# A two-layer streaming trunk: seven block products for eight in each projection group, and the plain eight

## The chip, the cores and the metric

The kernel runs on one core of one Trainium2 chip. The metric is the device time of one execution in microseconds (us); for a comparison, the median over several executions. Everything is computed in fp32. Where a product must be exact to nearly fp32, an operand is split into a high part in the fast fp32r format and a low part that holds the rest, and three matmuls (high x high, high x low, low x high) make one product.

## The reference

256 rows of 2048 numbers pass through two layers. Layer A is chunked attention with a relative-position bias; layer B is attention with a forget gate and a causal mask, against keys and values made from the stream once. Both gate the result with SiLU and project it back.

```python
D_MODEL, SEQ, D_INNER, N_HEADS, HEAD_DIM = 2048, 256, 4096, 32, 128
# layer A
h = rms_norm(x, a_norm[0])
q, k, v, g = jnp.split(h @ a_w_in[0], 4, axis=-1)        # 2048 -> 4 x 4096
o = chunked_relbias_attention(q, k, v, a_rel_bias[0])    # 64-row chunks, own and earlier ones
x = x + (o * jax.nn.silu(g)) @ a_w_out[0]                # 4096 -> 2048
# shared keys and values, forget gates
h_kv = rms_norm(x, kv_norm)
k_sh, v_sh = jnp.split(h_kv @ kv_w, 2, axis=-1)
cum_logf = jnp.cumsum(jax.nn.log_sigmoid(h_kv @ f_w + f_b), axis=1)
# layer B
q, g = jnp.split(rms_norm(x, b_norm[0]) @ b_w_in[0], 2, axis=-1)
o = forgetting_attention(q, k_sh, v_sh, cum_logf)        # causal
x = x + (o * jax.nn.silu(g)) @ b_w_out[0]
return rms_norm(x, final_norm)
```

## The kernel before

The weights are streamed once, in units of 512 output columns. A unit holds 16 slices of 128 rows of the inner dimension (32 in the output projections), taken two at a time: a sub-block is 256 x 512 numbers, 512 KB. `Feed` brings them: `load` starts the transfer on SP's queue into one of three raw buffers (`RAW`), `prepare` makes the high part on ScalarE (ACT) and the low part on VectorE (DVE) into one of four pairs of split buffers (`SPLIT`), and `get` hands a pair to TensorE (PE), with up to three pairs made ahead (`DEPTH`). `Unit.step` then multiplies: two slices, two halves of 128 rows of x, three matmuls each, so 12 matmuls of 128 x 512 for a sub-block, accumulated in two PSUM banks.

Both layers run over 16 groups of two heads (`NG`), two units for a group. In layer A these are aqk (queries and keys) and avg (values and gates); in layer B bqg (queries and gates, from `b_w_in`) and bkv (keys and values, from `kv_w`). The output projections ao and bo (`project`) stand behind the layers.

From the second group of each layer on, the units have only seven sub-blocks (`QUAD * KB` slices). The eighth sub-blocks of the two units of a group form a quad: two slices of two units against two halves of rows, which is a 2 x 2 block matrix times another, done in seven block products in place of eight. `Quads` holds what is needed. `load_quad` fetches both raw sub-blocks ahead of time, ordered by a dummy activation (`behind`); `differ` forms differences of weight blocks on DVE (in layer B it scales them by the gain on ACT first); `quad` splits four tiles of such combinations on ACT and DVE; `sums_of_x` forms the sums of x once per layer; `products` issues the seven products (21 matmuls) behind the third step of the group's first unit, four into banks of their own (p1, p5, p6, p7), and combines them on DVE and ACT into the tile `comb`. When a unit ends, `first_half` (L650) and `whole_sums` (L656) add `comb` to the accumulators on DVE. The first group of each layer has plain units of eight sub-blocks, whose evacuation is `evac_scaled` on ACT (L414).

Attention is a generator, cut by `yield` into segments that `drive` calls between the steps of the units, so that the work of one group lies beside the matmuls of the next. Its parts, in order:

- `turn(qk)`: a DVE transpose (L405) and 16 small transfers (L408) from POOL's queue, in layer A four of them from ACT's; target is `home`, a space inside the quad's tiles
- the split of keys and queries (wide, q1, q0) on ACT and DVE
- s1p and s0p: scores on PE, then the softmax on DVE and ACT, in two segments
- gates and `turn(sg)`: four activations, a transpose, 16 transfers on POOL's queue into sgZ
- the split of the probabilities (wideh on ACT L427, widel on DVE L428), ordered by a dummy activation behind the split of a coming sub-block (`line`)
- op: values times probabilities on PE (L435 to L437, L493)
- oT: gate and split of the result

Step tables say behind which sub-block a segment is called: in layer A `PV7_STEPS` and `QK7_STEPS`, in layer B `B1_STEPS` and `B2_STEPS`. `drive` also takes the generator of the group before that (`old`): one segment (the split of the probabilities) is called behind step 0, and everything left, op first, behind step 1. PE works in this written order: it cannot pass an op that waits. On the other engines the order is set when the program is laid out, near the order of the calls, and is fixed on the chip.

## Time and profile before

| | us |
|---|---|
| median of three runs | 1816.73 |
| lowest and highest run | 1811.34, 1823.83 |
| the profiled execution, whole | 1826.52 |
| its span, first to last instruction | 1824.8 |
| PE busy in it | 1771.9 |
| DVE busy | 1420.1 |
| ACT busy | 1184.8 |
| POOL busy | 522.0 |

The stages of the span: the first group of layer A to about 53.7 us, its 15 quad groups to 730.7, the first output projection to 899.1, the first group of layer B to 948.2, its 15 quad groups to 1640.3, and the second output projection with the final norm to 1824.8. The granted TensorE clock has a mean of 0.988 of full speed over the execution.

A row of a timeline gives start, length, engine, line, operation, output and inputs, shape and count; a bracket tells how long the engine stood idle before it and for whom. A row of the waits gives the waiting instruction, the one that released it, the sum in us, how often, and the longest. A line can be that of a helper: L184 is every unit's matmul, L435 to L437 every product of three.

### The profile page before, as it was taken

Reading aid. Unit: us, or ns where it says so; the run is one execution under the profiler, and the core shown is the slowest. Engines: PE = TensorE matmul, PEld = TensorE weight load, DVE = VectorE, ACT = ScalarE, POOL = GpSimd, SP = SyncE. Lnnn points to the kernel's source line nnn. Section 1 sums busy time; section 2 is a strip of 40 time slices with the busy share of each in tenths; the row PEclk is TensorE's granted clock in tenths of the full one; section 3 lists DMA queues with packets and bytes.
Section 4 is the critical chain, followed back from the end, with each engine's and each line's share of the span. In section 5 each row is a group of like instructions: output and inputs, shape, how many; then the busy total and the mean of one; then the engine's idle time right before and its main releaser. Section 6 shows DMA issues by size and latency. Waiting matters only on the chain.

```text
span 1824.8 us, 26015 instructions
## 1 busy us (share of the span) xinstructions
PE 1771.9 (97%) x8297; PEld 1534.1 (84%) x8297; DVE 1420.1 (78%) x2094; ACT 1184.8 (65%) x2245; POOL 522.0 (29%) x1071
## 2 busy tenths in 40 slices
PE   9999999999999999999999999999999999999997
PEld 7888888888888888888888888888888888888886
DVE  7888888888887787665668888888888889886554
ACT  6666666666566566554557877777777778765443
POOL 1333333333333333222014333333333333333000
PEclk9999999999999999999999999999999999999999
DMA  8776676666666666677756666666666666666664
GB/s 276 224 226 218 216 227 218 219 218 224 219 217 214 219 204 204 211 242 246 234 188 217 216 215 216 218 215 215 215 216 213 213 209 219 206 224 215 214 213 159
DMA packets 151337, 396.38 MB, mean 217 GB/s; under 512 B 31104, under 2 KB 38560, under 8 KB 151072
## 3 DMA queue, kind: packets, MB, share of 16 engines
q1 hardware_dynamic: 115152, 354.25, 59.4%
q0 software_dynamic: 32256, 37.29, 6.7%
q10 hardware_dynamic: 3792, 3.17, 0.6%
q8 instruction: 66, 1.08, 0.3%
q14 instruction: 71, 0.58, 0.1%
HBM read 351.05 MB, written 4.23 MB: 195 GB/s over the span
## 4 chain that ended last, share of the span: by engine, by line
PE 29%; DMA 13%; DVE 12%; ACT 7%; issue 4%; POOL 0%; ACTq 0%; SPq 0%; DVEq 0%
PE ao_acc L184 8%; PE bo_acc L184 7%; PE bqg_acc L184 6%; DMA bkv_raw<-in_kv_w 4%; DVE bqg_lo L241 3%; DMA bqg_raw<-in_b_w_in 3%; DVE bkv_lo L241 2%; PE bkv_acc L184 2%; ACT bkv_hi L240 2%; DMA cb<-cumd 2%; ACT bqg_hi L240 1%; DVE quad_lo L286 1%; DVE qk L650 1%; DMA bo_raw<-in_b_w_out 1%; PE op L493 1%
## 5 line engine op out<-in xcount | busy, mean ns | idle before, releaser
L408 POOL DMA_DIRECT2D sgZ<-sgY x512 | 251.4, 498 | 510.6 <-issue 245.9
L245 ACT ACTIVATE avg_hi<-avg_raw 128x1024 fp32r<-128x1024 f32 x112 | 118.3, 1056 | 137.9 <-DMA avg_raw<-in_a_w_in 88.7
L241 DVE SCALAR_TENSOR_TENSOR bkv_lo<-bkv_raw,gain,bkv_hi 128x512 fp32r<-128x512 f32 x226 | 159.2, 743 | 44.9 <-ACT bkv_hi L240 44.8
L246 DVE TENSOR_TENSOR avg_lo<-avg_raw,avg_hi 128x1024 fp32r<-128x1024 f32 x112 | 136.7, 1220 | 59.1 <-ACT avg_hi L245 59.0
L241 DVE SCALAR_TENSOR_TENSOR bqg_lo<-bqg_raw,gain,bqg_hi 128x512 fp32r<-128x512 f32 x226 | 163.5, 770 | 14.7 <-ACT bqg_hi L240 14.4
L240 ACT ACTIVATE bqg_hi<-bqg_raw,gain 128x512 fp32r<-128x512 f32 x226 | 148.4, 710 | 38.1 <-DMA bqg_raw<-in_b_w_in 27.7
L184 PE MATMUL bqg_acc<-bqg_hi,x1Th 128*128 128x512 f32 x452 | 173.0, 394 | 0.0
L184 PE MATMUL bqg_acc<-bqg_lo,x1Th 128*128 128x512 f32 x452 | 169.6, 387 | 0.0
L184 PE MATMUL bqg_acc<-bqg_hi,x1Tl 128*128 128x512 f32 x452 | 169.4, 386 | 0.0
L184 PE MATMUL aqk_acc<-aqk_hi,xTh 128*128 128x512 f32 x452 | 168.3, 384 | 1.0 <-ACT aqk_hi L245 1.0
L240 ACT ACTIVATE bkv_hi<-bkv_raw,gain 128x512 fp32r<-128x512 f32 x226 | 149.8, 711 | 29.4 <-DMA bkv_raw<-in_kv_w 26.0
L184 PE MATMUL avg_acc<-avg_hi,xTh 128*128 128x512 f32 x452 | 168.0, 383 | 0.0
L184 PE MATMUL aqk_acc<-aqk_lo,xTh 128*128 128x512 f32 x452 | 166.8, 381 | 1.2 <-DVE aqk_lo L246 1.2
L184 PE MATMUL aqk_acc<-aqk_hi,xTl 128*128 128x512 f32 x452 | 166.8, 381 | 0.0
L184 PE MATMUL avg_acc<-avg_lo,xTh 128*128 128x512 f32 x452 | 166.6, 380 | 0.0
L184 PE MATMUL avg_acc<-avg_hi,xTl 128*128 128x512 f32 x452 | 166.5, 380 | 0.0
L184 PE MATMUL bkv_acc<-bkv_hi,x1Th 128*128 128x512 f32 x452 | 166.3, 379 | 0.0
L184 PE MATMUL bkv_acc<-bkv_hi,x1Tl 128*128 128x512 f32 x452 | 166.1, 379 | 0.0
L184 PE MATMUL bkv_acc<-bkv_lo,x1Th 128*128 128x512 f32 x452 | 166.1, 379 | 0.0
L408 POOL DMA_DIRECT2D b_sums<-b_quad x256 | 125.7, 499 | 137.9 <-issue 62.6
L246 DVE TENSOR_TENSOR aqk_lo<-aqk_raw,aqk_hi 128x1024 fp32r<-128x1024 f32 x110 | 131.9, 1222 | 41.1 <-ACT aqk_hi L245 40.9
L408 POOL DMA_DIRECT2D sums<-quad x192 | 94.5, 499 | 195.1 <-PE op L493 173.3
(318 smaller groups left out, 4392.6 us busy)
## 6 DMA issues: line engine op xcount, KB each, us to landing
bqg_raw<-in_b_w_in SPq DMA_DIRECT2D x113, 512.0 KB, 4.2
bkv_raw<-in_kv_w SPq DMA_DIRECT2D x113, 512.0 KB, 4.7
avg_raw<-in_a_w_in SPq DMA_DIRECT2D x112, 512.0 KB, 5.6
aqk_raw<-in_a_w_in SPq DMA_DIRECT2D x110, 512.0 KB, 4.0
ao_raw<-in_a_w_out SPq DMA_DIRECT2D x64, 512.0 KB, 4.1
bo_raw<-in_b_w_out SPq DMA_DIRECT2D x64, 512.0 KB, 4.2
sgZ<-sgY POOLq DMA_DIRECT2D x512, 40.0 KB, 4.0
quad<-in_a_w_in SPq DMA_DIRECT2D x32, 512.0 KB, 6.2
```

The costliest lines, as they stand in the source:

```text
L184: pe.matmul(acc[t], x[:, t * P:(t + 1) * P], w, start=t not in begun, stop=k == nk - 1 and i == 2)
L240: act.activation(hi[:, :, j], raw[:, :, j], AF.Copy, scale=gk)
L241: dve.scalar_tensor_tensor(lo[:, :, j], raw[:, :, j], gk, r32(hi[:, :, j]), op0=OP.mult, op1=OP.subtract)
L245: act.activation(hi[:, :, j], raw[:, :, j], AF.Copy)
L246: dve.tensor_sub(lo[:, :, j], raw[:, :, j], r32(hi[:, :, j]))
L286: dve.tensor_sub(lo[:, :, :n], src, r32(hi[:, :, :n]))
L408: queues[j].dma_start(out=r32(z)[j * SQ:(j + 1) * SQ, i], in_=y[i * SQ:(i + 1) * SQ, j])
L493: pe.matmul(op[:, i, P:], v1[:, i * DH:(i + 1) * DH], pT[:, i, NT], start=False, stop=i == HG - 1)
L650: dve.scalar_tensor_tensor(dst[:, t], acc[t][:, :dst.shape[-1]], rs[:, t:t + 1], self.comb[:, i0 + t, :dst.shape[-1]], op0=OP.mult, op1=OP ...
```

## The change

The quads go in both layers. All units have eight sub-blocks, and `Feed` knows only these: `load_quad`, `differ`, `quad` and the class `Quads` are left out, with their big tiles. One tile, `turned`, takes over the space that `turn(qk)` used inside the quads' tiles, for both layers. All groups evacuate with `evac_scaled` on ACT, and the v and gate parts are read from PSUM directly. The step tables are written for eight steps, and `drive` takes a table for the older generator too: in layer A op is now called behind step 2, in layer B still behind step 1.

```diff
-PV_STEPS = {0: 1, 7: 1}
-QK7_STEPS = {0: 1, 5: 1, 6: 2}
-PV7_STEPS = {0: 1}
-B1_STEPS = {2: 1, 3: 1, 5: 2}
-B2_STEPS = {0: 1}
+PV_STEPS = {1: 1}
+OLD_A_STEPS = {0: 1, 2: 99}
+B1_STEPS = {3: 1, 5: 1, 6: 2}
+B2_STEPS = {1: 1}
+OLD_B_STEPS = {0: 1, 1: 99}
+FORGET_STEPS = {0: 1, 2: 1, 6: 1, 7: 1}
...
-        nk = KD if g == 0 else QUAD * KB
-        qkvg.append(spec(f"aqk{g}", a_w_in[2 * g], nk))
-        qkvg.append(spec(f"avg{g}", a_w_in[2 * g + 1], nk))
+        qkvg.append(spec(f"aqk{g}", a_w_in[2 * g], KD))
+        qkvg.append(spec(f"avg{g}", a_w_in[2 * g + 1], KD))
...
+    turned = big_tile([P, 2, NQ, 2 * HG * NT, SQ], F32, name="turned")
+    home = [turned[:, i] for i in range(2)]
...
         qk = rows(UN, "qk")
-        if g:
-            qa.first_half(qk, accs["qk"], 0, rsA)
-        else:
-            evac_scaled(accs["qk"], 0, UN, rsA, qk)
+        evac_scaled(accs["qk"], 0, UN, rsA, qk)
...
-    def drive(gen, side, steps, hooks={}, old=None, last=0):
+    def drive(gen, side, steps, hooks={}, old=None, old_steps={}):
         acc = None
         for i, acc in enumerate(gen):
-            finish(old) if i >= last else advance(old)
+            advance(old, old_steps.get(i, 0))
             advance(side, steps.get(i, 0))
...
-            first, second = (Unit(xT, next(order)) for _ in range(2))
-            accs["qk"] = drive(rest(first), prev, PV7_STEPS,
-                               {QUAD_STEP - 1: lambda: qa.products(first, second, (rsA, [(t, UN) for t in range(NT)])),
-                                LOAD_STEP: lambda: g + 1 < NG and feed.load_quad("a", g + 1)})
-            vg = rest(second)
+            accs["qk"] = drive(unit(xT), prev, PV_STEPS)
+            vg = unit(xT)
...
-        accs["vg"] = drive(vg, prev, QK7_STEPS, {0: lambda: g + 1 < NG and feed.differ("a")}, old, 1)
-        if not g:
-            qa.sums_of_x()
+        accs["vg"] = drive(vg, prev, QK_STEPS, {}, old, OLD_A_STEPS)
...
-    project(oA, ao_order, ao_begun, ao_closed, [(prev, [1, 7, 1, 1])])
+    project(oA, ao_order, ao_begun, ao_closed, [(prev, [2, 6, 2, 1])])
...
-        if g:
-            qb.first_half(qk[:, :, GC:], kv, NT, rsB)
-            kv = qb.whole_sums(kv, NT, GC)
-        else:
-            evac_scaled(kv, 0, GC, rsB, qk[:, :, GC:])
+        evac_scaled(kv, 0, GC, rsB, qk[:, :, GC:])
...
-        accs["qg"] = drive(rest(first), prev, B1_STEPS, hooks, old, 1)
-        hooks = {2: lambda: open_b(accs), 3: lambda: more and feed.differ("b")}
-        accs["kv"] = drive(rest(second), prev if g else fg, B2_STEPS if g else {1: 1, 3: 1, 6: 1, 7: 1}, hooks)
+        accs["qg"] = drive(unit(x1T), prev, B1_STEPS, {}, old, OLD_B_STEPS)
+        accs["kv"] = drive(unit(x1T), prev if g else fg, B2_STEPS if g else FORGET_STEPS, {2: lambda: open_b(accs)})
...
-    project(oB, bo_order, bo_begun, bo_closed, [(old, [1, 1, 0]), (prev, [3, 1, 1, 1, 1, 7, 1, 1])])
+    project(oB, bo_order, bo_begun, bo_closed, [(old, [1, 1, 0]), (prev, [4, 2, 1, 1, 1, 7, 2, 1])])
```

`QK_STEPS = {0: 1, 6: 1, 7: 2}` stands in both versions; only the new one uses it.

149 lines of the change are left out of this document (15 added, 134 removed).

## The prediction

> **What bounds the kernel.** I read the page's busy shares first, then the stages (windows), the waits of PE, and the timelines of PE, DVE and ACT around the longest wait.
>
> ```profile
> PE 1771.9 (97%) x8297; PEld 1534.1 (84%) x8297; DVE 1420.1 (78%) x2094; ACT 1184.8 (65%) x2245; POOL 522.0 (29%) x1071
> ```
> ```profile
> 53.70:730.70 677.00, 666.02 (x3139) 575.76 (x3137) 549.47 (x732) 420.14 (x763) 208.98 (x435) 0.99 0.68 217
> ```
> ```profile
> 948.20:1640.30 692.10, 668.46 (x3129) 581.37 (x3127) 595.35 (x991) 530.40 (x1117) 252.98 (x509) 0.98 0.65 214
> ```
>
> The two windows are the 15 quad groups of each layer (columns: length, then busy time of PE, PEld, DVE, ACT, POOL, granted clock, DMA share, GB/s). PE is called 97% busy, but the matmul rows overlap, so that share hides lost time. The price of a matmul is the distance between starts; in the kv unit below (first row to the first row of the next unit) 84 matmuls follow one another without a gap.
>
> ```profile
> 1296.10 0.59 PE L184 MATMUL bkv_acc<-bkv_hi,x1Th 128*128 128x512 f32 x2
> ...
> 1314.23 0.59 PE L184 MATMUL bqg_acc<-bqg_hi,x1Th 128*128 128x512 f32 x2
> ```
>
> (1314.23 - 1296.10) / 84 = 0.2158 us, not the 0.38 us that a single row lasts. The attention matmuls of the same group, in program order inside the qg unit:
>
> ```profile
> 1319.41 0.28 PE L435 MATMUL op<-wideh,vh 128*128 128x256 f32 x1
> 1320.36 0.39 PE L436 MATMUL op<-widel,vh 128*128 128x256 f32 x1 [0.67 <-DVE widel L428]
> 1320.59 0.28 PE L437 MATMUL op<-wideh,vl 128*128 128x256 f32 x1
> 1320.70 0.28 PE L435 MATMUL op<-wideh,vh 128*128 128x256 f32 x1
> 1321.30 0.39 PE L436 MATMUL op<-widel,vh 128*128 128x256 f32 x1 [0.32 <-DVE widel L428]
> 1321.52 0.28 PE L437 MATMUL op<-wideh,vl 128*128 128x256 f32 x1
> 1321.73 0.68 PE L493 MATMUL op<-sgZ,v 128*128 128x128 f32 x4
> 1322.17 0.46 PE L184 MATMUL bqg_acc<-bqg_hi,x1Th 128*128 128x512 f32 x1
> ```
> ```profile
> 1337.14 0.28 PE L435 MATMUL s1p<-wideh,q1h 128*128 128x256 f32 x1
> ...
> 1338.21 0.46 PE L184 MATMUL bqg_acc<-bqg_hi,x1Th 128*128 128x512 f32 x1
> ```
>
> s1p and s0p take 1.07 us. op takes 2.76 us, of which 0.95 - 0.11 and 0.60 - 0.11 (0.11 is the unhindered step, 1320.59 to 1320.70) are waits for DVE's widel: 1.43 without them. So a quad group's PE work is 189 x 0.2158 + 1.07 + 1.43 = 43.3 us. Layer B takes 692.1 / 15 = 46.1 per group, so it loses 2.9 (43 us in all); layer A takes 677.0 / 15 = 45.1 and loses 1.8 (28 us). Where the loss sits:
>
> ```profile
> PE op L436 <- DVE widel L428: 22.9, 25, 2.6
> ```
> ```profile
> PE op L436 <- DVE widel L428: 3.0, 6, 1.0
> PE s0p L459 <- ACT aqk_hi L245: 2.3, 9, 0.3
> PE op L435 <- ACT wideh L427: 2.2, 3, 1.2
> ```
>
> These are PE's waits in the B window (first fence) and the A window (second). op waits in B more than four times as long as in A (22.9 against 3.0 + 2.2), though it stands at the same place in both, behind two sub-blocks. DVE shows why:
>
> ```profile
> 1316.19 0.47 DVE L650 SCALAR_TENSOR_TENSOR qk<-bkv_acc,rstd_b,b_comb 128x256 f32<-128x256 f32 x1
> 1316.59 0.41 DVE L656 TENSOR_TENSOR b_comb<-bkv_acc,b_comb 128x256 f32<-128x256 f32 x1
> 1316.92 0.47 DVE L650 SCALAR_TENSOR_TENSOR qk<-bkv_acc,rstd_b,b_comb 128x256 f32<-128x256 f32 x1
> 1317.31 0.41 DVE L656 TENSOR_TENSOR b_comb<-bkv_acc,b_comb 128x256 f32<-128x256 f32 x1
> 1317.64 1.23 DVE L405 STREAM_TRANSPOSE b_quad<-qk 128x1024 f32<-128x1024 f32 x1
> 1318.80 1.18 DVE L286 TENSOR_TENSOR quad_lo<-b_quad,quad_hi 128x1024 fp32r<-128x1024 f32 x1
> 1319.90 0.41 DVE L428 TENSOR_TENSOR widel<-sgZ,wideh 128x256 fp32r<-128x256 f32 x1
> 1320.24 0.68 DVE L288 TENSOR_TENSOR b_quad<-b_quad 128x512 f32<-128x512 f32 x1
> 1320.84 0.41 DVE L428 TENSOR_TENSOR widel<-sgZ,wideh 128x256 fp32r<-128x256 f32 x1
> ```
> ```profile
> 1315.97 0.72 ACT L427 ACTIVATE wideh<-sgZ 128x256 fp32r<-128x256 f32 x2
> ```
>
> ACT had both halves of wideh by 1316.69; DVE began widel at 1319.90 because quad work stood ahead of it without a gap. The B waits are thus DVE's backlog, and that backlog is the quads'. They also cost clock:
>
> ```profile
> 1267.20:1296.10 28.90, 27.32 (x126) 0.94 0.50 159
> 1314.20:1340.90 26.70, 25.71 (x127) 1.00 0.54 169
> ```
> ```profile
> 998.90:1002.40 3.50, 3.50 (x12) 2.99 (x12) 3.00 (x6) 1.57 (x3) 3.50 (x9) 0.51 0.26 70
> ```
>
> Two qg units of B (length, PE, clock, DMA): one with a drop of the granted clock, one without. A drop is one stretch of about 3.4 us at half clock (last row), so 1.7 us each. The B stage's mean of 0.98 says (1 - 0.98) x 692 = 14 us, eight drops.
>
> **The change, part by part.** *Matmuls.* In each of 30 groups eight block products of three matmuls each stand in for seven: 3 x 0.2158 = 0.65 us more, 19.4 us in all, and all of it lies on PE, the path that sets the end. By the duration in the rows (0.38) it would be 34; that is the upper end, and the pitch is nearer, since PE never waited in those 84.
>
> The Trainium skill, "TensorE: Matmul & The Clock Gate", section "Back-to-back issue gap", gives about 131 ns as the sustained price of a load-and-multiply stream of 512 columns and 216 ns for the isolated one. By the first the term would be an estimated 11.8 us; the measured 0.2158 bears out the second, so this is set aside.
>
> *DVE and ACT work.* Out of DVE's row ahead of widel go both L650, both L656, quad_lo and L288: 2 x (0.39 + 0.33) + 1.10 + 0.60 in pitch from start to start, 3.1 us; 2.5 of it stood ahead of the first widel. In comes the lo pair of an ordinary sub-block, about what quad_lo took (1.1 to 1.3). So the first widel starts between 1317.4 and 1318.7 in this group, and op wants it at 1319.5. The evacuation moves to ACT:
>
> ```profile
> L414 ACT ACTIVATE qk<-bkv_acc,rstd_b x2: 475/475/475, 947.6 to 948.4; 128x256 f32<-128x256 f32 x2
> ```
>
> that is 2 x 0.48 us at the unit's start, where two hi splits of quads go and one of a sub-block comes: nothing net on ACT. The eighth sub-block passes through the ordinary ring of three raw buffers and four split ones; the bytes from HBM are the same, and SP's two quad loads per group become two raw loads. I cost these edits at nothing on PE; what hides them is the lead of the split buffers, and without that cover the second or third rival comes.
>
> *Moved steps.* The turn of sg goes from behind step 0 to behind step 1 in both layers: four ACT gates, a DVE transpose and 16 POOL issues, which no other POOL work stands behind but the next qk turn.
>
> ```profile
> L408 POOL DMA_DIRECT2D sgZ<-sgY x512 | 251.4, 498 | 510.6 <-issue 245.9
> ```
>
> The issues take 16 x 0.5 = 8 us. To the split there are seven sub-blocks, 18 us (in A 8.75 before, with the products; in B the same seven): enough by several us, cost nothing. The s1p steps keep one to two sub-blocks behind their split, and qk's turn gets at least the room it had. Cost nothing; a late one would show as s1p waiting for q1h.
>
> *op in layer B* stays behind step 1, its split behind step 0. The gate that orders the split (behind) hangs on the split of sub-block 3 in place of the quad's first. That is the arrangement layer A has now. So I take A's loss there: 3.0 + 2.2 us of idle time in 15 groups is 0.35 per group; with PE's restart 0.5. Ends: 0 (widel comes 2.5 us earlier, at 1317.4, and op wants it at 1319.5) and the whole 2.9. The drops hang on waits of about 2 us and more, so I leave 2 of 8. B: -(43 - 15 x 0.5 - 3.5) = -32, and +9.7 for the matmuls: -22.
>
> *op in layer A* moves behind step 2, 12 matmuls (2.6 us) later than now; the longest wait there is 1.2. Its 5.2 us of idle go, with restarts and clock about 9 (ends 5 and 28); what is queued behind op on PE is the next sub-block, which needs nothing of it, and oT on DVE and ACT comes 2.6 us later, a whole group ahead of its reader. The s0p wait stays: its split keeps its distance of one step. A: -9 + 9.7 = +1.
>
> *The ends.* In the last projection s1p now waits:
>
> ```profile
> PE s1p L435 <- ACT q1h L427: 1.9, 1, 1.9
> ```
>
> Its split goes from step 4 to 6 and the wait with it, with one clock drop: -3. Group 0 of layer A has only seven steps left in its second unit, so the entry for step 7 finds none: its s1p slips behind step 1 of the next unit, and its split of p and op come together behind step 2, with the gate on a sub-block prepared in the same step. Once: 0 to +5, I take +2.
>
> *Sum*: -22 + 1 - 3 + 2 = -22 us (by the ends: from 19.4 - 43 - 28 - 3 = -55 to 19.4 + 5 = +24). The profiled execution took 1826.5 us around its span of 1824.8; the median of the runs shown, 1816.7, lies 10 us below it. By proportion and by difference the median becomes 1795.
>
> **The rivals.** *The wait changes hands* (other side). The gate now needs a fresh raw transfer, where the quad's raw had landed long before. If sub-block 3 is late, wideh is late and op waits in B as it does now. It decides once wideh comes 5 us after the unit's start (here 1.7, 1315.97 - 1314.23): with its own 0.7, one transpose and widel (1.2 + 0.4) the split then ends at 7.3, and op, which stands at 5.2, waits the 2 us that it waits on the mean now. At that mark only A's 9 and the ends' 1 come back: 1816.7 + 19.4 - 10 = 1826; each 0.5 us later adds 15 x 0.5, so 1841 at 6. For it: A's op waits on ACT wideh three times. Against: most of A's groups don't wait.
>
> *The ring binds.* Sixteen sub-blocks per group go through three raw buffers, for fourteen now:
>
> ```profile
> avg_raw<-in_a_w_in SPq DMA_DIRECT2D x112, 512.0 KB, 5.6
> ```
> ```profile
> L245 ACT ACTIVATE avg_hi<-avg_raw 128x1024 fp32r<-128x1024 f32 x112 | 118.3, 1056 | 137.9 <-DMA avg_raw<-in_a_w_in 88.7
> L246 DVE TENSOR_TENSOR avg_lo<-avg_raw,avg_hi 128x1024 fp32r<-128x1024 f32 x112 | 136.7, 1220 | 59.1 <-ACT avg_hi L245 59.0
> ```
>
> A buffer's turn is 5.6 + 1.06 + 1.22 = 7.9 us, a third of it 2.63; PE eats a sub-block in 12 x 0.2158 = 2.59 and pauses 2.5 per group, so 16 x 2.63 = 42.1 against 43.9: just enough. From a turn of 8.2 us it binds; at 8.6 a group takes 45.9, 2 us more: 1795 + 60 = 1855. Against it: the transfers of the quads, which crowd the same queue, go.
>
> *The drops stay.* The clock falls for another reason than the waits: the 10 us that I let go stay, 1795 + 10 = 1805, or 1809 if the last drop stays too and waits come with them.
>
> The Trainium skill speaks for that rival: the same page, "Part 1: The HAM clock gate", lets the clock fall only after an idle window of about 3.4 us, and no wait here is that long (2.6 at most). The trace does not agree: the drops sit in the units with the long waits, as in the two rows shown.
>
> **How the numbers follow.** About 1% is what a measurement of this kernel can tell from no change. The forecast (1777 to 1804 by itself) has 0.52; the wait that changes hands 0.20; the drops that stay 0.13; the ring 0.15. Faster by over 1% (below 1798.6): four fifths of the forecast, 0.44, and a little of the ring's and the drops' cases, 0.46; slower (over 1834.9): a third of the second case and half of the ring's, 0.15; between, 0.39. The range of 8 in 10, 1777 to 1840, leaves out what of the forecast is better still and the ring's upper half.
>
> **What would show it.** PE's waits in B: op on widel falls from 22.9 to under 8 us; the clock of the B stage rises to 0.99 or 1.00; A's op waits are gone. The pitch of matmuls stays 0.2158, with about 8,390 of them. DVE's busy time falls. It would be wrong if PE's unit matmuls begin to wait for lo or hi (the ring), or if widel, late with wideh, still ends behind op's place.

## The result and the profile after

| | us | against the kernel before, 95% interval |
|---|---|---|
| before, median of the runs beside it | 1819.6 | |
| after, median of four runs (1759.16 to 1762.96) | 1761.73 | 0.9677 [0.9644, 0.971] |
| predicted | 1795 (1777 to 1840) | |

The change makes the kernel 58 us faster, where 22 were predicted; the time lies below the predicted range. (In the runs further down, one execution of dve2 out of five took 3101 us at a granted clock of 0.56; it is left out of that run's ratio.) The page of the kernel after, its busy times (engine, us, share of the span, instructions):

```profile
PE 1746.0 (99%) x8387; PEld 1533.1 (87%) x8387; DVE 1159.1 (66%) x1662; ACT 1084.1 (62%) x2063; POOL 515.7 (29%) x1071
```

The two windows of the 15 later groups of each layer (length, then busy time of PE, PEld, DVE, ACT, POOL, granted clock, DMA share, GB/s):

```profile
51.20:711.60 660.40, 658.38 (x3191) 580.46 (x3191) 426.91 (x548) 390.88 (x703) 208.52 (x435) 1.00 0.72 225
926.20:1581.40 655.20, 655.20 (x3173) 577.94 (x3172) 471.47 (x773) 466.30 (x1017) 249.42 (x512) 1.00 0.72 228
```

Layer A falls from 677.0 to 660.4 us (-16.6) and layer B from 692.1 to 655.2 (-36.9). The second projection with the norm goes from 184.5 to 179.0 (-5.5), the rest (start, first projection, first group of B) by 5.4: together the 64.4 us between the two spans, 1824.8 and 1760.4. The clock column is 1.00 in both windows: the drops of the two layers are gone. So are nearly all of PE's waits. The whole list of PE's waits in the execution after:

```profile
PE op L390 <- ACT wideh L382: 1.9, 1, 1.9
PE heat L108 <- DVE zeros L105: 1.3, 1, 1.3
PE aqk_acc L182 <- DVE aqk_lo L238: 1.2, 2, 0.9
PE bo_acc L182 <- DVE bo_lo L238: 0.8, 1, 0.8
PE avg_acc L182 <- DVE avg_lo L238: 0.3, 1, 0.3
```

No op waits for widel, no s0p and no s1p waits for anything; the one op that waits is the one of group 0 of layer A. The timeline around op in a later group of layer B (start, length, engine and line):

```profile
1275.11 0.59 PE L182 MATMUL bqg_acc<-bqg_hi,x1Th 128*128 128x512 f32 x2
...
1277.13 0.72 ACT L382 ACTIVATE wideh<-sgZ 128x256 fp32r<-128x256 f32 x2
...
1278.27 0.75 DVE L383 TENSOR_TENSOR widel<-sgZ,wideh 128x256 fp32r<-128x256 f32 x2
...
1280.29 0.28 PE L390 MATMUL op<-wideh,vh 128*128 128x256 f32 x1
...
1280.41 0.28 PE L391 MATMUL op<-widel,vh 128*128 128x256 f32 x1
...
1281.36 0.46 PE L182 MATMUL bqg_acc<-bqg_hi,x1Th 128*128 128x512 f32 x1
```

widel is done at 1279.02, 1.3 us before op starts, and op takes 1.07 us (1280.29 to 1281.36) where it took 2.76. What else moved is seen one step further up, at the split of the weights. ACT's idle time ahead of the weights' high parts (columns as on the page's list of groups: busy, mean ns, idle before and what ended it), first before, then after:

```profile
L240 ACT ACTIVATE bqg_hi<-bqg_raw,gain 128x512 fp32r<-128x512 f32 x226 | 148.4, 710 | 38.1 <-DMA bqg_raw<-in_b_w_in 27.7 <-PE ao_acc L184 5.3 <-PE bkv_acc L184 3.1
L240 ACT ACTIVATE bkv_hi<-bkv_raw,gain 128x512 fp32r<-128x512 f32 x226 | 149.8, 711 | 29.4 <-DMA bkv_raw<-in_kv_w 26.0 <-PE bqg_acc L184 3.0 <-PE bkv_acc L184 0.4
```
```profile
L232 ACT ACTIVATE bqg_hi<-bqg_raw,gain 128x512 fp32r<-128x512 f32 x256 | 170.9, 714 | 114.1 <-PE bqg_acc L182 50.2 <-PE bkv_acc L182 37.1 <-DMA bqg_raw<-in_b_w_in 16.0
L232 ACT ACTIVATE bkv_hi<-bkv_raw,gain 128x512 fp32r<-128x512 f32 x256 | 168.8, 711 | 27.9 <-PE bqg_acc L182 21.4 <-PE bkv_acc L182 5.8 <-DMA bkv_raw<-in_kv_w 0.6
```

Before, the split waited for the raw block (DMA, 53.7 of 67.5 us): in layer B the stream of weights ran behind. After, it waits for PE to give a split buffer back (114.5 of 142.0 us): the stream runs ahead as far as its four buffers let it. I call the distance from the end of a slice's low part on DVE to the first matmul that uses it the lead. Two DVE timelines around a unit's start show it; the first is of the kernel before, in the group whose unit starts at 1314.23, the second of the kernel after:

```profile
1308.32 0.82 DVE L524 SCALAR_TENSOR_TENSOR gs<-gs,b_comb 128x256 f32<-128x256 f32 x2 [0.26 <-ACT gs L523]
1309.06 0.75 DVE L241 SCALAR_TENSOR_TENSOR bkv_lo<-bkv_raw,gain,bkv_hi 128x512 fp32r<-128x512 f32 x1
1309.72 1.22 DVE L274 TENSOR_TENSOR b_quad<-b_quad 128x1024 f32<-128x1024 f32 x1
1310.86 0.75 DVE L241 SCALAR_TENSOR_TENSOR bqg_lo<-bqg_raw,gain,bqg_hi 128x512 fp32r<-128x512 f32 x1
1311.53 0.68 DVE L275 TENSOR_TENSOR b_quad<-b_quad,b_quad 128x512 f32<-128x512 f32 x1
1312.13 4.14 DVE L241 SCALAR_TENSOR_TENSOR bqg_lo<-bqg_raw,gain,bqg_hi 128x512 fp32r<-128x512 f32 x5
```
```profile
1268.57 1.41 DVE L233 SCALAR_TENSOR_TENSOR bqg_lo<-bqg_raw,gain,bqg_hi 128x512 fp32r<-128x512 f32 x2 [0.91 <-ACT bqg_hi L232]
1271.28 1.41 DVE L233 SCALAR_TENSOR_TENSOR bqg_lo<-bqg_raw,gain,bqg_hi 128x512 fp32r<-128x512 f32 x2 [1.30 <-ACT bqg_hi L232]
1274.23 1.42 DVE L233 SCALAR_TENSOR_TENSOR bqg_lo<-bqg_raw,gain,bqg_hi 128x512 fp32r<-128x512 f32 x2 [1.54 <-ACT bqg_hi L232]
```

Before, the first slice of the unit is split at 1310.86 + 0.75 = 1311.61, 2.6 us ahead of PE, and three sub-blocks follow each other in DVE's queue without a gap, up to the evacuation and widel of the prediction's rows. After (unit start 1275.11), the same sub-block is done by 1269.98, 5.1 us ahead, and DVE stands idle between the sub-blocks.

### The profile page after: what moved, and what is told of

The parts are those of the page before. It is cut to its first block, busy times and chain, and to the rows that moved or that the text cites. A ratio compares the mean times of both kernels' runs of the same rounds, so it can differ in the third digit from the quotient of the medians.

```text
span 1760.4 us, 25526 instructions
## 1 busy us (share of the span) xinstructions
PE 1746.0 (99%) x8387; PEld 1533.1 (87%) x8387; DVE 1159.1 (66%) x1662; ACT 1084.1 (62%) x2063; POOL 515.7 (29%) x1071
## 4 chain that ended last, share of the span: by engine, by line
PE 94%; DMA 2%; DVE 2%; ACT 1%; issue 0%; POOL 0%; SPq 0%; ACTq 0%; DVEq 0%; POOLq 0%
PE bkv_acc L182 19%; PE bqg_acc L182 19%; PE avg_acc L182 18%; PE aqk_acc L182 17%; PE ao_acc L182 9%; PE bo_acc L182 8%; DMA bo_raw<-in_b_w_out 1%; PE op L448 1%; PE s0p L414 1%; PE op L391 0%; PE s1p L390 0%; PE s1p L391 0%; PE op L392 0%; PE op L390 0%; PE s1p L392 0%
## 5 line engine op out<-in xcount | busy, mean ns | idle before, releaser
L363 POOL DMA_DIRECT2D turned<-turned x448 | 219.9, 498 | 267.7 <-PE avg_acc L182 93.0
L232 ACT ACTIVATE bqg_hi<-bqg_raw,gain 128x512 fp32r<-128x512 f32 x256 | 170.9, 714 | 114.1 <-PE bqg_acc L182 50.2
L182 PE MATMUL aqk_acc<-aqk_hi,xTh 128*128 128x512 f32 x512 | 190.9, 383 | 0.2
L182 PE MATMUL aqk_acc<-aqk_lo,xTh 128*128 128x512 f32 x512 | 189.0, 379 | 1.2 <-DVE aqk_lo L238 1.2
L182 PE MATMUL avg_acc<-avg_lo,xTh 128*128 128x512 f32 x512 | 188.9, 379 | 0.3 <-DVE avg_lo L238 0.3
L182 PE MATMUL bkv_acc<-bkv_hi,x1Th 128*128 128x512 f32 x512 | 189.0, 379 | 0.0
L182 PE MATMUL avg_acc<-avg_hi,xTl 128*128 128x512 f32 x512 | 188.8, 379 | 0.0
L182 PE MATMUL bkv_acc<-bkv_lo,x1Th 128*128 128x512 f32 x512 | 188.8, 379 | 0.0
L182 PE MATMUL bkv_acc<-bkv_hi,x1Tl 128*128 128x512 f32 x512 | 188.8, 379 | 0.0
L237 ACT ACTIVATE aqk_hi<-aqk_raw 128x1024 fp32r<-128x1024 f32 x125 | 131.5, 1052 | 91.9 <-PE avg_acc L182 44.0
```

What stands on the lines that cost most here:

```text
L182: pe.matmul(acc[t], x[:, t * P:(t + 1) * P], w, start=t not in begun, stop=k == nk - 1 and i == 2)
L232: act.activation(hi[:, :, j], raw[:, :, j], AF.Copy, scale=gk)
L237: act.activation(hi[:, :, j], raw[:, :, j], AF.Copy)
L363: queues[j].dma_start(out=r32(z)[j * SQ:(j + 1) * SQ, i], in_=y[i * SQ:(i + 1) * SQ, j])
```

## The experiments

Four theories were held against each other. Theory 1, the prediction's: the quads' vector work makes a backlog ahead of widel. Theory 2: the place of op is all. Theory 3: the quads' transfers make the raw blocks late. Theory 4, formed after the first runs: a quad's four short entries eat the lead. Medians and ratios are against the kernel before on the same chip.

| run | what it is | median us | ratio, 95% interval |
|---|---|---|---|
| room | before, the part behind op one step later | 1818.12 | 0.9947 [0.9921, 0.9973] |
| room2 | before, op one step later | 1799.26 | 0.9901 [0.9862, 0.9941] |
| nodiff | before without differences | 1818.43 | 1.0013 [0.9984, 1.0042] |
| noload3 | nodiff without the quads' transfers | 1775.39 | 0.9765 [0.9743, 0.9786] |
| noload2 | noload3 without one more subtraction | 1770.99 | 0.9704 [0.9673, 0.9735] |
| spread | before, transfers in four pieces | 1871.68 | 1.0302 [1.0247, 1.0358] |
| spread_room | spread, op one step later | 1857.51 | 1.0209 [1.0177, 1.0241] |
| early | before, transfers at the quad | 1849.26 | 1.0148 [1.0091, 1.0205] |
| quads_a | quads in layer A only | 1780.87 | 0.9794 [0.976, 0.9828] |
| op_a1 | after, op in A at its old place | 1763.53 | 0.9649 [0.9623, 0.9674] |
| dve2 | after + 2 DVE operations at op's split in B | 1771.59 | 0.969 [0.9661, 0.9718] |
| dve4 | after + 4 of them | 1771.91 | 0.9694 [0.9669, 0.9719] |
| dma | after + quad-like transfers in A | 1766.39 | 0.9716 [0.9684, 0.9747] |
| halves | after + short entries in B | 1765.09 | 0.9704 [0.9673, 0.9734] |
| vec | after + quad-like vector work in B | 1761.02 | 0.9681 [0.9651, 0.9712] |
| halves_v | both | 1776.71 | 0.9762 [0.9724, 0.9799] |
| all3 | both, and transfers | 1780.34 | 0.9766 [0.9734, 0.9797] |
| fix0 | after, a table for group 0 | 1760.12 | 0.9676 [0.9646, 0.9707] |

### The place of op

In room, the last argument of `drive` was raised:

```diff
-        accs["vg"] = drive(vg, prev, QK7_STEPS, {0: lambda: g + 1 < NG and feed.differ("a")}, old, 1)
+        accs["vg"] = drive(vg, prev, QK7_STEPS, {0: lambda: g + 1 < NG and feed.differ("a")}, old, 2)
...
-        accs["qg"] = drive(rest(first), prev, B1_STEPS, hooks, old, 1)
+        accs["qg"] = drive(rest(first), prev, B1_STEPS, hooks, old, 2)
```

> The kernel before, quads and all, with one thing changed: the op matmuls of the group before stand behind step 2 instead of step 1, in both layers. The waits for s0p, the quads' transfers and their vector work stay. Theory 1 (the quads' own work on VectorE makes the low half of the probabilities, widel, ready 6.5 to 8.9 us after the unit's start in layer B and 5.0 to 7.7 in layer A; op at about 7.7 then waits 0 to 1.2 us instead of 1 to 3, and the clock is no longer lowered in between): about 1771 us, 1763 to 1782. Theory 2 (the place of op is the whole story, quad work is harmless): all of the waits go, 1745 us or less, which would beat the kernel after the change. Theory 3 (the quads' transfers make the raw blocks late, and PE waits for weights wherever op stands): the waits move to the split weights and s0p, 1790 us or more.

The edit was not what that text says. `drive` calls one segment of the older group behind every step below that argument, so op, the second segment, stayed behind step 1 (in the trace it stands 5.2 us behind the unit's start as before) and only the split of its result moved. The 0.5% tells nothing of the theories. room2 keeps this edit and adds the line in `drive` that it needs:

```diff
-            finish(old) if i >= last else advance(old)
+            advance(old, 99 if i >= last else i == 0)
```

> The kernel before, quads and all, with op behind step 2 in both layers and nothing called behind step 1 (the run called room only moved what comes after op: there op stayed at 5.2 us after the unit's start). Now op stands at 7.7 us. Theory 1 (backlog of the quads' vector work delays widel, to 6.3 to 9.1 us in layer B and to 5.3 to 7.4 in layer A): the waits for widel fall from about 27 to under 8 us in all and most drops of the clock go; what remains are the smaller losses at s1p and s0p: 1775 to 1795. Theory 2 (the place of op is everything): 1750 or less, better than the kernel after. Theory 3 (late transfers of the quads): widel comes later with op, 1805 or more.

1%, by the ratio 18 us: 1799 lies just outside theory 1's range (1775 to 1795) and far from theory 2. The head of PE's list of waits in room2:

```profile
PE s1p L435 <- ACT q1h L427: 10.8, 9, 2.3
PE s1p L437 <- DVE q1l L428: 6.5, 2, 3.4
PE op L436 <- DVE widel L428: 2.8, 5, 1.1
```

The wait for widel falls as theory 1 has it, but 17 us of waits for the split of keys and queries stand in its place. Both splits are ordered behind splits of weights, so a late stream of weights makes one or the other late; giving op room only changes which one PE meets. The reverse, op in layer A back at its old place in the kernel after:

```diff
-OLD_A_STEPS = {0: 1, 2: 99}
+OLD_A_STEPS = {0: 1, 1: 99}
```

> The kernel after the change with the room in layer A taken back: op behind step 1 of the avg unit instead of step 2 (as it stood before). No quads. Theory 1: widel ends 3.9 us after the unit's start and op would start at about 5.2, so nothing waits: 1761.7 us, within 4. Theory 2 (room is what removes the waits): waits of 0.5 to 1 us in each of 15 groups come back, 1769 to 1776.

No change that the intervals can tell (0.9649 against 0.9677): with the stream ahead, the room that the change gave op in layer A is worth nothing.

### Vector work ahead of widel

In layer B, in front of the split of the probabilities (two operations in dve2, four in dve4):

```diff
...
+        if line[0] == 1:
+            for _ in range(2):
+                dve.tensor_sub(extra[0], r32(feed.ready[line[1]][0]), extra[0])
         ph, pl = split([pT[:, i, :NT] for i in range(HG)], "wide", line[1])
```

> The kernel after the change with two dummy VectorE subtractions (128x1024, about 1.15 us each by the quad rows of before) put ahead of widel in each of the 14 later groups of layer B; what is computed is the same. Theory 1: widel ends at 3.9 + 2.3 = 6.2 us, op at 5.2 waits 0.5 to 1 us in each group: about 1773 us (1768 to 1777), and the waits are too short to lower the clock, so its row stays at 1.00 in the layer. Theories 2 and 3 (place of op, transfers): no change, 1762. Weights late in place of op would show as waits for bqg_lo or bkv_lo.

> As the run with two dummy subtractions, with four of them (4.6 us of VectorE work ahead of widel in each of 14 groups of layer B). Theory 1: widel ends at about 8.5 us, op waits about 3 us in each group: 1761.7 + 14 x 3 = 1804 us without lowered clock; and if waits of 2 to 3 us are what lowers the clock, up to 14 drops of about 1.7 us more, 1804 to 1830, with drops in the clock row of layer B in the groups with the longest waits. If the clock has another reason: no drops, 1804. Theories 2 and 3: no change, 1762.

dve2 lands where theory 1 puts it, 8 us above op_a1, which ran beside it. dve4 does not add to it, and its DVE timeline shows why it is no larger dose:

```profile
1282.76 1.22 DVE L445 TENSOR_TENSOR extra<-bqg_hi,extra 128x1024 f32<-128x1024 f32 x1
1283.89 0.42 DVE L383 TENSOR_TENSOR widel<-sgZ,wideh 128x256 fp32r<-128x256 f32 x1
1284.23 1.22 DVE L445 TENSOR_TENSOR extra<-bqg_hi,extra 128x1024 f32<-128x1024 f32 x1
1285.36 0.42 DVE L383 TENSOR_TENSOR widel<-sgZ,wideh 128x256 fp32r<-128x256 f32 x1
1285.70 1.21 DVE L445 TENSOR_TENSOR extra<-bqg_hi,extra 128x1024 f32<-128x1024 f32 x1
```

The program's layout put one operation ahead of each half of widel, in dve2 too, and the other two of dve4 behind it. So the runs show that DVE work straight in front of widel, 1.1 us ahead of its first half and 2.3 ahead of its second, costs 0.6 us a group even on a full lead, and they show nothing on longer delays. Then the converse, the differences taken out of the kernel before:

```diff
-        accs["vg"] = drive(vg, prev, QK7_STEPS, {0: lambda: g + 1 < NG and feed.differ("a")}, old, 1)
+        accs["vg"] = drive(vg, prev, QK7_STEPS, {0: lambda: not g and feed.differ("a")}, old, 1)
...
-        hooks = {2: lambda: open_b(accs), 3: lambda: more and feed.differ("b")}
+        hooks = {2: lambda: open_b(accs), 3: lambda: not g and feed.differ("b")}
```

> The kernel before with the two subtractions between raw blocks of a quad (and in layer B the four ACT gains in front of them) left out from the third group of each layer on: the products then run on blocks that are not the differences, so the sums differ. In the DVE rows of before they take 1.14 + 0.60 us, 4 to 6 us ahead of widel, in one gapless run with it. Theory 1: widel ends 1.7 us earlier in layer B, where op waits 2 us on the mean, so about 14 x 1.5 us and most of the clock drops go there, and some of layer A's waits: 1785, 1775 to 1797. If only the work directly ahead of widel counts (my prediction's list): no change in B, 1810 or more. Theory 3 (transfers): no change, 1815.

No change, against theory 1 in the wide form that counts the differences. It is also what the expectation names for the case that only the work directly ahead of widel counts, which was the prediction's own list; nodiff leaves that list as it was and says nothing against it. The ACT timeline of nodiff ahead of the unit that starts at 1314.2 shows what took DVE's place:

```profile
1311.15 2.54 ACT L240 ACTIVATE bqg_hi<-bqg_raw,gain 128x512 fp32r<-128x512 f32 x4
1314.58 1.33 ACT L240 ACTIVATE bqg_hi<-bqg_raw,gain 128x512 fp32r<-128x512 f32 x2 [0.88 <-DMA bqg_raw<-in_b_w_in]
```

The third sub-block of the unit had not landed; its split, the evacuation and widel behind it came nearly as late as before. For the differences, then, DVE's gapless run was the last link of a chain that was late already.

### Short entries, vector work and transfers on a full lead

dma adds the quads' transfers to layer A of the kernel after, with a tile that nothing reads:

```diff
+    def crowd(g):
+        for r in range(2):
+            feed.behind(spare[0][:, r, :, 0, :1], -1)
+            sp.dma_start(out=spare[0][:, r], in_=a_w_in[2 * g + r][7])
...
-            accs["qk"] = drive(unit(xT), prev, PV_STEPS)
+            accs["qk"] = drive(unit(xT), prev, PV_STEPS, {5: lambda: crowd(g)})
```

> The kernel after the change with two more loads of 512 KB in each later group of layer A, at the place where the quads' loads stood, into a spare tile that nothing reads. Theory 3 (bursts of the quads' transfers make raw blocks late and caused layer A's waits): landing of avg_raw rises from 4.3 us to 5.5 or more, weights come late, waits of layer A come back: 1770 to 1785. Theory 1 (it was the quads' vector work): the transfers are hidden by the 4 to 6 us by which the split weights are ahead: 1762, within 5.

The head of PE's list of waits in dma:

```profile
PE op L390 <- ACT wideh L382: 4.9, 1, 4.9
```

The landing of avg_raw rose to 4.9 us, not to 5.5, and the 4.7 us by which the time rose sit at group 0's op, which now waits 4.9 us in place of 1.9, with one drop of the clock (6.8 us at half) around it. No other op, s0p or s1p waits.

halves cuts two sub-blocks of layer B's first unit into entries of one slice, each of which takes a whole pair of split buffers; vec adds vector work; halves_v is both:

```diff
+    def halved(name, b):
+        return name[:3] in ('bqg',) and name[3:] != "0" and b in (3, 4)
...
+            if halved(spec["name"], b):
+                j, self.half = self.half, 1 - self.half
+                self.prepare_half(spec, b, raw, j)
```
```diff
+        hooks = {0: lambda: vector_work(3, 0), 2: lambda: vector_work(4, 5)} if g else {}
-        accs["qg"] = drive(unit(x1T), prev, B1_STEPS, {}, old, OLD_B_STEPS)
+        accs["qg"] = drive(unit(x1T), prev, B1_STEPS, hooks, old, OLD_B_STEPS)
...
```

> The kernel after the change; in layer B from the second group on, sub-blocks 3 and 4 of the qg unit come to PE as two entries of one slice each, so that four entries of the split ring hold 24 matmuls where they otherwise hold 48 (a quad's four hold 21). Same splits, same transfers, same matmuls, nothing else of a quad. Theory 4, new (the quad's four short entries fill the ring of four and eat the lead of the split weights, 0.1 to 0.7 us behind each quad before the change, 4 to 6.6 after it; whatever is ordered behind a split is then late): the lead falls to under 1.5 us behind sub-block 4; if that alone makes op late, 1775 to 1795. Theory 1 (amount of vector work): 1762, within 5, the lead back at 4 us within four sub-blocks.

> The kernel after the change with dummy vector work in each later group of layer B, about as much as the quads' and at their places: 12 DVE subtractions of 128x512 (3 at op's split, 4 behind step 2 of the qg unit, 2 and 3 behind steps 2 and 3 of the kv unit; 7 to 8 us) and 9 ACT copies (about 4 us). DVE's busy time in layer B comes to about 580 us (595 before the change). No quads, full entries. Theory 1 (amount of vector work): most of layer B's loss comes back, 1785 to 1798. Theory 4 (short entries): the 4 to 6 us of lead hide it except what stands directly ahead of widel at op (as the runs with dummy subtractions showed, up to 10 us): 1762 to 1775.

> Both at once: the short entries of the run halves and the vector work of the run vec, in layer B. If the two are what a quad costs in waits, layer B loses what it lost before (2.4 us a group against now): 1790 to 1800, more than the two runs' gains and losses added up if they work together (short entries take the lead, vector work keeps it from coming back). If the cause is something else of the quads (their transfers, their bank use), under 1780.

By the medians halves costs 3 to 4 us (its interval overlaps that of the kernel after), vec nothing, the two together 15. That is under the 1780 which the expectation of halves_v named as the sign of another cause. The windows of layer B in vec and in halves_v:

```profile
925.40:1580.60 655.20, 655.20 (x3173) 577.96 (x3171) 570.82 (x953) 508.14 (x1152) 251.13 (x512) 1.00 0.72 227
```
```profile
926.70:1598.20 671.50, 665.11 (x3174) 581.15 (x3172) 576.37 (x953) 511.19 (x1152) 250.99 (x512) 1.00 0.71 222
```

The same DVE time (571 and 576 us, 471 after, 595 before) costs nothing where the entries are full and 16 us where two sub-blocks come short. That is an interplay, and it is less than half of the 37 us that layer B gained from the change. It is also another wait than that of the kernel before: in layer B of halves_v only s1p and s0p wait (5.5 us in all) and op does not. In both runs widel stands about where it stands in the kernel after (first half 3.2 us behind the unit's start in vec, 2.7 in halves_v, 3.2 after; medians), so they try vector work elsewhere in the group; the work ahead of widel was tried in dve2. all3 adds transfers to both:

```diff
-        hooks = {0: lambda: vector_work(3, 0), 2: lambda: vector_work(4, 5)} if g else {}
+        hooks = {0: lambda: vector_work(3, 0), 2: lambda: vector_work(4, 5), 5: lambda: crowd(g)} if g else {}
```

> The run halves_v (short entries and vector work in layer B, 1776.7) with two loads of 512 KB more in each later group of layer B, behind step 5 of the qg unit, into a tile that nothing reads: all that a quad costs outside PE. If the three work together on the lead, layer B loses what it lost before: 1790 to 1802. If transfers are hidden: 1774 to 1782.

No more than halves_v, by the ratios. Put into the kernel after, the transfers slow one raw block (the fifth of the second unit lands in 6.1 us in place of 4.4, medians), but the lead at the start of the next unit is 4.2 us against 4.6 in halves_v, and PE's waits do not grow. So the question goes back to the kernel before.

### The transfers in the kernel before

noload2 and noload3 leave out the quads' loads, on top of nodiff:

```diff
-                                LOAD_STEP: lambda: g + 1 < NG and feed.load_quad("a", g + 1)})
+                                LOAD_STEP: lambda: None})
...
-        hooks[LOAD_STEP] = lambda: more and feed.load_quad("b", g + 1)
+        hooks[LOAD_STEP] = lambda: not g and feed.load_quad("b", 1)
```

noload2 also leaves out `dve.tensor_sub(raw[:, :, 0, 1], ...)` in `quad`, the subtraction that stands on DVE between the two halves of widel.

> The kernel before with the quads' three kinds of side work on their blocks left out from the third group of each layer on: no loads of 2 x 512 KB a group, no differences (as in the run nodiff), no subtraction between two halves of a split. The products run on old blocks, so the sums differ. The four short entries and the sums behind the products stay. Beside nodiff (no change) this tells the share of the transfers. If the bursts are what makes the raw blocks late (ACT waits for raws 185 us in the kernel before, 21 in the one after): raws land sooner, widel is earlier, 1785 to 1805. If they are hidden and the short entries are what costs: 1810 to 1820.

> As nodiff (the differences between raw blocks left out from the third group of each layer on), and in addition without the quads' loads of 2 x 512 KB a group from that group on; unlike in noload2, the subtraction between two halves of a split stays. The products run on old blocks, so the sums differ. Beside nodiff (1818) it is the transfers alone. If they take the lead of the split weights: layer B at 43.5 to 44 us a group, 1771 to 1782 in all. If it was the subtraction that noload2 left out: 1805 or more.

Here the time goes: from nodiff to noload3 the ratio falls by 0.025, the medians by 43 us, with only the transfers (and the dummy activations that order them) gone. The one subtraction more of noload2 gives another 4 us by the medians and nothing between the two profiled spans (1773.2 and 1772.8). The windows of layers A and B, nodiff first:

```profile
52.80:729.10 676.30, 664.21 (x3137) 572.77 (x3136) 525.39 (x704) 418.84 (x763) 208.79 (x435) 1.00 0.68 217
949.30:1637.10 687.80, 664.93 (x3127) 577.87 (x3126) 570.13 (x963) 497.40 (x1060) 252.88 (x509) 0.99 0.65 214
```
```profile
53.90:719.00 665.10, 656.59 (x3138) 571.37 (x3136) 524.37 (x704) 414.91 (x735) 209.07 (x435) 1.00 0.63 199
936.10:1590.20 654.10, 650.70 (x3129) 570.97 (x3127) 567.72 (x963) 496.43 (x1033) 256.88 (x509) 1.00 0.64 203
```

Layer B loses 34 us, layer A 11. DVE has the same work in both (570 and 568 us in layer B). PE's wait for widel, 25.9 us over the kernel before and 22.9 of it in layer B, is nearly gone in noload3 (in layer B alone 1.3):

```profile
PE op L436 <- DVE widel L428: 4.4, 10, 1.1
```

The second half of widel ends 7.7 us behind the unit's start in the kernel before, 7.4 in nodiff, 5.4 in noload3 and 3.9 in the kernel after (medians of 14 groups, from the traces' rows; the first half starts at 6.4, 6.0, 4.1 and 3.2). So of the 3.8 us by which the change brings it forward, the transfers are worth about 2; the 1.5 between noload3 and the kernel after go with what is left of the quads, of which the evacuation and the quads' own splits on DVE stand straight ahead of widel.

The medians of the lead over the 15 groups of layer B, in us, for the first slice of each sub-block (worked out from the traces' rows as above; "|" is the place of the quad or, in halves_v, of the short entries' end):

```
            first unit (qg)                       second unit (kv)
before      2.5 2.5 6.9 | 1.4 2.6 3.9 4.1         4.1 5.2 4.6 3.2 2.6 3.5 3.4
nodiff      2.6 3.5 6.6 | 1.4 2.6 3.9 4.1         4.1 5.1 4.5 3.1 2.5 3.3 2.8
noload3     5.4 5.3 6.7 | 1.4 2.6 3.9 4.1         4.1 5.0 4.4 4.7 4.1 4.6 5.2
room2       2.4 2.9 2.8 | 1.0 1.6 2.9 3.1         3.1 4.3 3.7 2.7 2.1 3.2 3.0
early       3.3 4.3 6.9 | 1.3 2.6 3.8 1.6         2.4 3.7 2.8 2.4 3.6 2.9 2.7
spread      3.4 0.6 7.0 | 1.4 2.6 3.9 4.1         4.1 5.1 4.5 4.2 3.6 4.5 3.0
halves_v    4.6 5.2 6.2 6.2 4.6 | 1.7 3.0 4.8     4.8 5.3 6.0 3.9 5.0 4.5 3.9 3.8
after       6.1 6.1 7.1 6.3 6.9 7.2 6.1 7.1       6.2 7.2 7.2 5.0 6.1 5.6 5.5 6.1
```

With and without transfers (noload3 and nodiff) the rows agree from the quad's place up to the third sub-block of the second unit. Behind it the transfers take 1.3 to 2.4 us (nodiff beside noload3), which are not regained; the next unit begins with 2.6 us of lead in place of 5.4, and there widel is queued. (The third sub-block of the first unit stands behind op, so its lead holds op's time and wait.) The short entries take theirs in both: behind the quad the lead is down to 1.4 us with and without the transfers. Why the transfers hurt just there is seen in stretches of 4 us of the kernel before, in the group that starts at 1314 (DMA share and GB/s are the last two columns):

```profile
1320.00:1324.00 4.00, 3.32 (x18) 2.80 (x19) 4.00 (x8) 1.58 (x4) 4.00 (x9) 1.00 0.24 72
1324.00:1328.00 4.00, 4.00 (x20) 3.52 (x19) 2.61 (x5) 3.27 (x6) 3.25 (x7) 1.00 0.25 71
1340.00:1344.00 4.00, 4.00 (x20) 3.49 (x19) 2.61 (x7) 2.63 (x10) 0.00 (x0) 1.00 0.95 338
1344.00:1348.00 4.00, 4.00 (x20) 3.50 (x19) 2.93 (x4) 4.00 (x9) 0.00 (x0) 1.00 0.95 341
```

While the short entries hold the four split buffers, the raw ring stays full and the transfers rest for 8 us. When the stream then catches up, four raws and the two quad loads go out within 8 us and nearly fill the queues (0.95). The Trainium skill, "DMA: Bandwidth & Descriptors", section "Specifications", gives some 358 GB/s as the limit of one core from HBM; the 338 and 341 measured here agree that little was left.

The harm has two parts, which the issue and landing times of the raw blocks in the second unit tell apart (nodiff beside noload3, medians of 14 groups). The fourth and fifth raw blocks are issued 1.3 and 0.6 us after their buffers came free, behind quad loads that wait in SP's queue for their gate, where noload3 has 0.03; and the fourth to sixth blocks land in 4.7, 5.9 and 5.8 us, where noload3 has 3.4, 4.6 and 4.2. So for the fourth block the order in SP's queue costs as much as the slower transfer. No run takes one away and leaves the other.

If it is the place of the loads and not the amount, the burst should do less harm elsewhere. Two places were tried, with everything computed. spread sends four pieces of 256 KB behind steps 4 and 6 of the first unit and 1 and 3 of the second; spread_room adds op's later place; early sends both loads from within the products:

```diff
-                sp.dma_start(out=q.raw[:, :, r], in_=q.w(r, g))
+            sp.dma_start(out=q.raw[:, :, r, j], in_=q.w(r, g)[:, :, j])
...
+            self.behind(q.raw[:, :, r, j, :1], -1)
```
```diff
             w = feed.get()
+            load()
             prod(p1, x(0, 0), w, 0, True)
```

> The kernel before, complete, with the quads' loads in four pieces of 256 KB, behind steps 4 and 6 of the first unit and 1 and 3 of the second (it was 2 x 512 KB behind step 5), and the differences behind step 5 of the second unit. If it is the burst that takes the lead at one go: each piece costs 1.1 us of lead and is regained before the next, layer B at 44 to 45 us a group, 1780 to 1800. If it is the amount (the ring of three can't regain anything): 1810 to 1820, no gain.

> As spread, with op behind step 2 in both layers (as in room2, 1799). If burst and place of op are separate: 1765 to 1785. If the loss moves on to s1p as in room2: 1790 to 1800. Under 1760 it would beat the kernel after the change.

> The kernel before, complete, with one thing moved: the quads' two loads of 512 KB go out inside the quad's products, right behind the fetch of its first entry, instead of behind step 5. In the kernel before, the transfers stand at 0.24 to 0.25 of the queues' share for 8 us behind the quad (the ring is full of raws that wait for the short entries) and at 0.95 for 8 us when the quads' loads meet four raws. If it is the collision that takes the lead: it stays at 5 us through the second unit as in noload3, layer B at 43.6 to 44.5 us a group, 1775 to 1790 in all with every part of the quads computed. If it is the amount, or the loads wait for the short entries there too: 1810 to 1825.

All three are slower than the kernel before, by 1.5 to 3%, and none parts amount from place cleanly, because each brought a loss of its own. In early the loads wait at the head of SP's queue until the last split has read the quad's tile:

```profile
SPq L264 <- DVE quad_lo L286: 258.8, 28, 15.1
```

This wait costs the raw blocks next to nothing (in layer B they are issued 0.03 us after their buffers came free, in layer A 0.2 at one place). But the two loads then go out together with the three raw blocks that refill the ring behind the quad. These land in 6.1 to 6.2 us in layer B and 7.1 to 8.6 in layer A, where noload3 has 3.2 to 4.7 and 3.6 to 6.6: the same collision at a worse place. Layer A, where PE now waits for the split weights themselves, takes 695.9 us in place of 677.0.

In spread the gates wait too, 105.2 us in all where the kernel before has 34.6, and again the raw blocks are issued as their buffers come free (0.03 us at every place by the medians):

```profile
SPq L264 <- ACT b_quad L293: 34.6, 15, 2.9
```
```profile
SPq L268 <- ACT b_quad L302: 105.2, 59, 6.7
```

The loss comes from the differences, which had to move behind the last piece. ACT stands for the pieces (L281, 73 us of idle time in all, where the same operations have 5 in the kernel before), for the last one just ahead of the second sub-block of the next unit:

```profile
1392.64 0.72 ACT L281 ACTIVATE b_quad<-b_quad,gain 128x512 f32<-128x512 f32 x1 [2.25 <-DMA b_quad<-in_kv_w]
```

That sub-block's raw had landed 3.6 us before the unit's start, yet its lead is down to 0.6 us in the table, and widel comes late behind it (PE waits 49.0 us for it, where the kernel before has 25.9). Up to there the pieces had taken little: at the fourth to sixth sub-blocks of the second unit the lead is 4.2, 3.6 and 4.5 us, against 3.2, 2.6 and 3.5 before and 4.7, 4.1 and 4.6 without transfers. So spread speaks for the place, as far as it goes; a run that spreads the loads without holding ACT was not made, and what it would give stays open.

### The rest

quads_a keeps the quads of layer A and takes layer B from the kernel after:

> Quads in layer A only, as before the change; layer B as after it. By the windows of the two kernels layer A gave 16.6 us of the 64 and the start and ao some 4. If the layers are independent: 1761.7 + 17 to 21 = 1779 to 1783, with layer B at 43.7 us per group. If the gain was the work of one layer alone (B), 1765; if of what both share, over 1790.

As expected for independent layers: by the medians quads cost layer A 19 us and layer B the other 38. Last, a table for group 0:

```diff
-        accs["vg"] = drive(vg, prev, QK_STEPS, {}, old, OLD_A_STEPS)
+        accs["vg"] = drive(vg, prev, QK_STEPS if g else {0: 1, 5: 1, 6: 2}, {}, old, OLD_A_STEPS)
```

> The kernel after the change with group 0 of layer A given a table for its seven steps (a segment behind steps 0 and 5, two behind 6), so that its probabilities are split before op asks for them: the three waits of op on wideh (4.8 us in the trace after, partly under the steps) go, -2 to -4: 1758 to 1760. If s1p of group 0 waits in its place: 1762.

The one wait of op is gone from the list, and the median is 1.6 us lower, which the intervals (0.9676 against 0.9677) do not tell from the kernel after. (The 4.8 us and "three waits" of that expectation added up the columns of one row, which are sum, count and longest: it is one wait of 1.9.)

## Why the prediction was right in direction and wrong in size

- *Matmuls, +19.4.* Right. In the kernel after, a kv unit's 96 matmuls run from 1254.39 to 1275.11, 0.2158 us each, and a group of layer B takes 655.2 / 15 = 43.68 us, where 192 x 0.2158 + 1.07 + 1.07 is 43.57.

```profile
1254.39 0.59 PE L182 MATMUL bkv_acc<-bkv_hi,x1Th 128*128 128x512 f32 x2
...
1275.11 0.59 PE L182 MATMUL bqg_acc<-bqg_hi,x1Th 128*128 128x512 f32 x2
```

- *The floor of a quad group, 43.3.* Too high: op without waits takes 1.07 us, not the 1.43 that was left when the two waits, from start to start, were taken off the waiting one. A wait also cost PE in the steps behind it (0.2 in place of 0.11 us). So layer B lost 46.1 - 42.9 = 3.2 a group instead of 2.9, some 5 us in all, and by the same floor layer A as much more.
- *The stream, "I cost these edits at nothing on PE".* This is the step that failed most. It put the quads' loads at nothing, and they were the largest single cost: 43 us by noload3, 34 of them in layer B and 11 in layer A by the windows. They held the stream of weights back, so that in layer B the lead at the start of the first unit, where widel is queued, was 2.6 us in place of 5.4 (nodiff and noload3), and widel came 2 us later.
- *op in layer B, -32 and a rest of 11.* Too small. "So I take A's loss there" gave 0.5 us a group and two drops that should stay. Nothing stayed: no wait for widel, clock 1.00, and -36.9 net instead of -22, which is 46.6 before the 9.7 for the matmuls. The reason given for the gain, DVE's quad work ahead of widel, was the smaller part of the chain. Its own size seems about right: the prediction let widel start 1.2 to 2.5 us earlier by it, and between noload3 and the kernel after widel starts 0.9 us and ends 1.5 us earlier. Taking these off the medians of the kernel before leaves the first half of widel ready at 5.9 us, where op wants it at 5.3: an estimated wait of 0.6 us a group, about the rest that was predicted. What the reason left out is the 2 us of the transfers. No run takes away the work ahead of widel alone, so what it is worth by itself is not shown.
- *op in layer A, -9, with the matmuls +1.* Failed too: -16.6, the one-off of group 0 included, so 26 us went in place of 9. "The s0p wait stays: its split keeps its distance of one step" looked at steps. The split stands behind a split of weights, and with these ahead the wait went with the rest, at op's old place too (op_a1). 11 of the 26 us go with the transfers; the rest was not taken apart.
- *The ends, -3 and +2.* The wait of s1p in the last projection went, -5.5 with what hung on it. Group 0's op waits once for wideh, 1.9 us, as worked out.
- *Moved steps and the evacuations, nothing.* Right: no wait for sgZ, qk or q1h in the list.
- *The rivals.* The wait that changes hands: wideh begins 2.0 us behind the unit's start (1277.13 - 1275.11), far from the 5 us that decide. The drops that stay: none is left in the layers. The ring that binds: it does not bind in the kernel after, where avg_raw lands in 4.3 us in place of the 5.6 of the prediction's row. But the crowding of the transfer queue that it names was there before, and it was a large part of what the change removed. I set it down as an "against", and did not price it as a gain.

```profile
avg_raw<-in_a_w_in SPq DMA_DIRECT2D x127, 512.0 KB, 4.3
```

The four misses (layer B 15, layer A with its group 0 20, the last projection 2.5, the stages that I held constant 5.4) make up the 42 us between the predicted and the measured difference of the profiled executions, -22 and -64. The floor's share is inside the first two. The -64 lies below even the sum of the good ends, -55, so the range had no room for it. The direction was forecast for a reason that was only a part of it; that the cost which was not on the list lay on the same side was luck. (One slip on the way: four fifths of the forecast's 0.52 are 0.42 and not 0.44, which changes nothing here.)

Shown is: the quads' transfers are worth some 43 us in the kernel before, of the 77 that the quads cost beside the 19 that they save; its differences nothing; on a full lead each of the quad's side works costs 0 to 5 us, short entries and vector work together 15, and up to 2.3 us of DVE work straight ahead of widel 8. Not shown is how the other 34 us divide between short entries and the vector work ahead of widel, how much of the transfers' harm is order in SP's queue and how much slower transfer, and how much another place for them could save.

## What to carry to other kernels

Work that is queued behind a prefetch stream inherits the stream's lead, so measure that lead (end of preparation to first use) at each point of the loop before pricing a wait; the instruction that PE waits for can be the last of a late chain, as widel was here. Small entries in a ring cost its depth in time, and a side stream that shares the queue can then take what is left, though the mean load of the queue is moderate (0.65 in layer B before). When the cause of lateness goes, a neighbouring stage that has the same cause is no measure of the rest: here nothing was left.

## What the runs showed of the hardware

- A waiting op cost PE more than its idle brackets: 2.76 us with 0.99 of brackets against 1.07 without a wait, so 0.7 us beside them. About half of it is wait that the brackets leave out, since a bracket begins at the end of a row of 0.28 us where the unhindered step is 0.11; the other half is slower steps behind each wait.
- DVE stood at 570.8 of 655.2 us (87%) in layer B of vec with no loss at all, and at 595 of 692 (86%) before with 3.2 us lost in a group: its busy share alone told nothing of the loss.
- Behind long waits of op PE often runs at half speed. In the kernel before, op takes 2.2 to 4.0 us longer than without waits in ten groups, and nine of these have a drop of the clock of 3.4 us there; the other 22, at most 1.8 us longer, have none. It is no sharp limit: op of group 0 in the kernel after takes 2.7 us longer and has no drop. In the group that starts at 1267, with waits of 1.26 and 0.32 us in brackets, the steps that follow are 0.43 us, twice 0.2158.

```profile
1276.58 0.63 PE L184 MATMUL bqg_acc<-bqg_lo,x1Th 128*128 128x512 f32 x1
1277.01 0.63 PE L184 MATMUL bqg_acc<-bqg_hi,x1Tl 128*128 128x512 f32 x1
1277.43 0.63 PE L184 MATMUL bqg_acc<-bqg_hi,x1Th 128*128 128x512 f32 x1
```
